# Two-layer hybrid encoder step on one core: second layer's projection ends on values, its raw weights share buffers with the softmax weights, the first head's scores move beside it, cached keys load a block ahead, the sample's steps start later

## The chip, the cores and the metric

The kernel is one program on one core of a Trainium2 chip. The metric is the device time of one execution in microseconds, here the median of three runs. The engines are named as the profile names them: PE (matmul and transpose), DVE (vector), ACT (scalar), POOL, and SP, which here only issues transfers; its queue takes them in order.

## The reference, cut to what matters

The kernel runs two layers of an encoder over 16 meta tokens, 1024 prompt tokens and 32 tokens of a running stream (the sample), 1072 columns of width 1024 in all. Every layer is a mixer and an MLP. The change lies in the second layer's mixer, a forgetting attention with 16 heads of 64:

```python
q, k, v, lf = c_project(hp, w_in_c[i], b_f_c[i], qnorm_c[i], knorm_c[i])   # h @ w_in, q and k normalised per head
xp = xp + fox_prompt(q, k, v, lf) @ w_out_c[i]                              # causal, 1040 keys
q, k, v, lf = c_project(hs, w_in_c[i], b_f_c[i], qnorm_c[i], knorm_c[i])
xs = xs + fox_sample(q, k, v, lf, cache_c_k[i], cache_c_v[i], cache_c_logf[i]) @ w_out_c[i]   # 1024 cached keys + 32
# both: s = q.k * SCALE + c_q - c_k, c = cumsum(log forget);  p = softmax(s);  o = p @ v
```

The arithmetic is float32. A product is made of three matmuls on a high and a low part of each operand (`mm3`), or of two where one stacks both parts.

## The kernel before, in words

**Order of the program.** Layer 1, its MLP, `project_c` (the second layer's projection), `fox` (its attention with the output product), the second MLP. Inside `fox` and the MLPs the order on PE is the order of the code. In `project_c` every engine's order, and everywhere the order on the other engines and of the transfers, comes from a scheduler that runs when the program is built.

**Before the projection.** The last quarter of the columns is normalised at its very end: squares on ACT, sums on DVE and POOL, one matmul with a constant (`normed`, L145), two activations, and then for eight blocks a scaling on DVE (L217), a high part on ACT (L64) and a low part on DVE (L66) or POOL (L68), through four buffers `nm_t`. They lie in a pool that is closed when this is done. `fh0`, the pool of the first head, is opened next, and above it `pc`, the pool of the projection, each on memory that earlier pools have left. A tile's first writer waits for the last readers of what lay there before.

**The projection.** Seven groups of columns of `w_in_c`, in the order of the list `cols`: values of heads 12 to 15 with the forget gates, q and k of heads 0 to 7, two groups of values of six heads, q and k of heads 8 to 15. For each group four transfers bring raw weights (`pj_raw`, three buffers), ACT and DVE split them (`pj_wh`, `pj_wl`), and for each of nine column tiles 24 matmuls go to one of four PSUM banks. Then `post_norm` (q, k: square, reduce, `rstd`, scale, gain on POOL, four transposes, split, out to DRAM) or `post_v` (copy, split, out to DRAM). Step n is group times nine plus tile. At step 9 `forget_sums` makes the running sums of the forget gates: transposes, a scan on DVE, and two halves that are split and sent out, once for the prompt and once for the sample. At step 45 head 0 is loaded, at steps 56, 58, 60, 62 its first four `head_scores` are made (matmuls, `softmax` with max on DVE, exp on ACT, division on POOL).

**The attention.** A head has two quads of four query blocks; quad 0 has 5 steps, quad 1 has 9, so 14 steps a head. A step transposes a block of weights (`head_weights`, L1490) and multiplies the block of two steps before with the values (L1500, L1501). From step 5 on the scores of the next head are made, one a step (L1472, L1473, L1476); in head 0 steps 0 to 3 also make its own scores 4 to 7. The sample's attention is cut into 53 pieces (`smp`), one a step from step 4 of head 0: `keys` loads 512 cached keys into the single buffer `fk_c` and transposes them. Heads 0, 2, ... lie in `fh0`, heads 1, 3, ... in the pool `fh`, which reuses the memory of the projection's pool. Each takes seven transfers for queries and keys (`fh_qa`, `fh_ka`, `fh_qb`, `fh_kb`) and two for values.

Of the kernel before, what the change touches and what calls it, by code (L numbers as in the profile page):

```python
# [8 lines left out]
F32 = mybir.dt.float32  # L9
F32R = mybir.dt.float32r  # L10
# [3 lines left out]
ALU = mybir.AluOpType  # L14
# [4 lines left out]
P = 128  # L19
# [32 lines left out]
class Core:  # L52
# [177 lines left out]
    def project(self, w, cols, sb, hT, lag, part, width=512, bufs=(3, 5)):  # L230
# [3 lines left out]
        for n, (a, b, post, bank) in enumerate(cols):  # L234
            ws = []
            for k in range(0, KB, 2):
                raw = sb.tile([P, 2, width], F32, name="pj_raw", bufs=bufs[0])
                wh = sb.tile([P, 2, width], F32R, name="pj_wh", bufs=bufs[1])
                wl = sb.tile([P, 2, width], F32R, name="pj_wl", bufs=bufs[1])
                nc.sync.dma_start(raw[:, :, :b - a], wv[:, k:k + 2, a:b])  # L240
                self.hi_lo(raw[:, :, :b - a], wh[:, :, :b - a], wl[:, :, :b - a])
                ws += [(wh[:, j, :b - a], wl[:, j, :b - a]) for j in range(2)]
# [936 lines left out]
    def project_c(self, hT, beside):  # L1179
        tc, nc, i, o = self.tc, self.nc, self.i, self.o  # L1180
        with tc.tile_pool(name="pc", bufs=2, reuse_waits="tile") as sb, tc.tile_pool(name="pcp", bufs=4, space=PSUM, reuse_waits="tile") as ps:
# [33 lines left out]
            def post_v(h0, nh, gates):  # L1215
                def post(t, r0, m, pp):
# [6 lines left out]
                    if gates:  # L1223
# [26 lines left out]
                (2048, 2432, post_v(0, 6, False)), (2432, 2816, post_v(6, 6, False)),  # L1250
                (512, 1024, post_norm(gq, self.zq1, 8, None)), (1536, 2048, post_norm(gk, self.zk1, 8, "new_c_k")),
            ]
            steps = self.project(w, [(*c, banks(ps)) for c in cols], sb, hT, 0,
                                 lambda: sb.tile([P, 512], F32, name="hn_sq"), bufs=(3, 4))
            for n, _ in enumerate(steps):
                if n == len(TILES):
                    with tc.tile_pool(name="pf", bufs=1, side="right", reuse_waits="tile") as sf:
                        self.forget_sums(sf)
                if n in beside:
                    beside[n]()  # L1260


    def forget_sums(self, sb):
# [9 lines left out]
        for dst, parts in ((self.cp, prompt), (self.cs, sample)):  # L1273
# [9 lines left out]
            for a in range(0, n, n // 2):  # L1283
                hl = [sb.tile([16, 528], F32R, name=f"fs_{x}")[:, :n // 2] for x in "hl"]
                self.hi_lo(d[:, a:a + n // 2], *hl)
                for x in range(2):
                    nc.sync.dma_start(dst[x, :, a:a + n // 2], hl[x].bitcast(F32))


    def softmax(self, sb, pieces, p, n):  # L1290
        nc = self.nc
        nm = sb.tile([P, 2], F32, name="sm_nm", bufs=4)
        den = sb.tile([P, 2], F32, name="sm_den", bufs=4)
        for j, (s, a, b) in enumerate(pieces):
            nc.vector.tensor_reduce(nm[:, j:j + 1], s, axis=AX.X, op=ALU.max, negate=True)
        if len(pieces) == 2:
            nc.vector.tensor_tensor(nm[:, 0:1], nm[:, 0:1], nm[:, 1:2], op=ALU.min)
        for j, (s, a, b) in enumerate(pieces):
            nc.scalar.activation(p[:, a:b], s, AF.Exp, bias=nm[:, 0:1], accum_out=den[:, j:j + 1])
        if len(pieces) == 2:  # L1300
            nc.vector.tensor_tensor(den[:, 0:1], den[:, 0:1], den[:, 1:2], op=ALU.add)
# [5 lines left out]
    def fox_sample(self, sb, work, ms):  # L1307
# [15 lines left out]

        def keys(g, a, p):
            def go():
# [132 lines left out]
    def head_scores(self, qi, d, sb, ps=None):  # L1458
# [19 lines left out]
        p = sb.tile([P, 1040], F32, name="fx_p1", bufs=6) if qi > 3 else self.fh0.tile([P, 528], F32, name="fx_p0", bufs=4)  # L1478
# [25 lines left out]
    def fox(self, d0, p0, ms, norm):  # L1504
        tc, nc, i = self.tc, self.nc, self.i
        w = i["w_out_c"][0]
        with ExitStack() as st:
# [3 lines left out]
            with tc.tile_pool(name="fh", bufs=2, reuse_waits="tile") as sb, tc.manual_schedule(engines={mybir.EngineType.PE}):  # L1511
# [16 lines left out]
                d, pr = {0: d0}, {(0, 0): p0}  # L1528
# [49 lines left out]
                for u, (h, quad) in enumerate(units):  # L1578
                    for t in range(4 * quad + 5):
                        step = 5 * quad + t  # L1580
                        if h == 14 and step == 0:
                            for n, names in enumerate((("fk_c", "fk_h", "fk_l"), ("fx_s", "fx_cs", "fv_c"))):
                                raw, wh, wo = (ssb.tile([P, 2, 512], F32R if x else F32, name=y, bufs=1) for x, y in enumerate(names))
# [3 lines left out]
                        if h == 0 and step < 4:  # L1587
                            scores(0, 4 + step)
# [3 lines left out]
                        if smp and (h or step >= 4):  # L1592
                            smp.pop(0)()
# [34 lines left out]
def body(tc, i, o):  # L1628
    C = Core(tc, i, o)
    nc = tc.nc  # L1630
    with ExitStack() as st:
# [215 lines left out]
```

## Time and profile before

| | |
|---|---|
| runs, us | 2826.71, 2821.92, 2815.38; median 2821.92 |
| profiled execution, us | 2817.04, span 2815.3 |
| granted PE clock, mean | 0.969 |
| PE / DVE / ACT / POOL busy | 93% / 67% / 45% / 23% |
| projection on PE | 1288.0 to 1607.4 us of the span |
| attention on PE, first to last product with values | 1625.0 to 2051.3 us |

The profiled execution lies 4.88 us below the median of the runs. In rows of the timeline the columns are start and duration in us, engine, line, operation, output and inputs, count, and in brackets the idle time before it and what ended it. In a table by windows, `(x..)` counts instructions and PEclk is the granted clock of PE as a share of full speed.

### The profile page before, as it was taken

The numbers are of one execution on the slowest core, as the hardware profiler recorded it, in microseconds if no ns is written. First come the engines' busy times: TensorE is split into PE (matmuls) and PEld (weight loads), VectorE is DVE, ScalarE is ACT, GpSimd is POOL, SyncE is SP. The second block draws the span as 40 slices with busy tenths as digits, with TensorE's granted clock in tenths as the row PEclk, the third lists the DMA queues.
The fourth block names the chain that finished last, engine by engine and source line by source line (L and its number), as shares of the span: only waits on it lengthen the run. The fifth ranks groups of instructions, "written<-read, shape, count | busy, mean of one in ns | idle before, by whom it ended". The sixth has DMA issues, their size and how long they took to land.

```text
span 2815.3 us, 49213 instructions
## 1 busy us (share of the span) xinstructions
PE 2624.8 (93%) x18391; PEld 2437.4 (87%) x18391; DVE 1892.2 (67%) x3850; ACT 1266.0 (45%) x2833; POOL 634.5 (23%) x693
## 2 busy tenths in 40 slices
PE   5899999869999999999999888999968999999998
PEld 5888988769999899998798766778868999999998
DVE  5934478786766686677634556778788767677553
ACT  4345465443333354545333356666653333335342
POOL 3423365110000211012201244555510000111000
PEclk9999999989999999999999989999989999999999
DMA  6343242225443766544464555444232344586643
GB/s 194 101 134 105 74 149 58 75 87 160 128 155 128 279 207 202 145 132 130 131 207 134 145 144 133 98 101 98 63 92 96 130 154 141 180 269 210 195 142 104
DMA packets 358038, 394.82 MB, mean 140 GB/s; under 512 B 41567, under 2 KB 294200, under 8 KB 355752
## 3 DMA queue, kind: packets, MB, share of 16 engines
q1 hardware_dynamic: 340840, 306.55, 38.2%
q0 software_dynamic: 16960, 85.13, 8.4%
q8 instruction: 145, 2.38, 0.4%
q14 instruction: 93, 0.76, 0.1%
HBM read 264.99 MB, written 125.48 MB: 139 GB/s over the span
## 4 chain that ended last, share of the span: by engine, by line
PE 75%; DVE 11%; DMA 4%; ACT 2%; issue 2%; POOL 1%; SPq 0%; DVEq 0%; ACTq 0%; POOLq 0%
PE bank L75 12%; PE bank L76 12%; PE bank L77 12%; PE mu_y L76 8%; PE mu_y L77 8%; PE mu_y L75 8%; PE bank L1490 3%; PE bank L1500 2%; PE bank L1501 1%; DMA md_ur<-ud 1%; PE fx_s L1472 1%; PE fx_s L1473 1%; PE bank L257 1%; DMA md_raw<-in_w_down 1%; DVE xT L878 1%
## 5 line engine op out<-in xcount | busy, mean ns | idle before, releaser
L75 PE MATMUL bank<-pj_wh,h 128*128 128x384 f32 (+3 forms) x832 | 300.1, 363 | 9.8 <-ACT pj_wh L64 7.4
L77 PE MATMUL bank<-pj_wh,h 128*128 128x384 f32 (+3 forms) x832 | 297.4, 359 | 6.1 <-DVE h L66 4.8
L76 PE MATMUL bank<-pj_wl,h 128*128 128x384 f32 (+3 forms) x832 | 298.5, 360 | 3.0 <-DVE pj_wl L66 2.9
L76 PE MATMUL mu_y<-md_u,md_w 128*128 128x268 f32 (+1 forms) x896 | 259.9, 290 | 13.3 <-DVE md_u L66 11.3
L77 PE MATMUL mu_y<-md_u,md_w 128*128 128x268 f32 (+1 forms) x896 | 259.4, 290 | 6.1 <-POOL md_w L68 6.1
L75 PE MATMUL mu_y<-md_u,md_w 128*128 128x268 f32 (+1 forms) x896 | 260.7, 291 | 0.3 <-ACT md_u L64 0.2
L75 PE MATMUL bank<-md_u,md_w 128*128 128x268 f32 (+1 forms) x896 | 257.3, 287 | 0.0
L76 PE MATMUL bank<-md_u,md_w 128*128 128x268 f32 (+1 forms) x896 | 255.9, 286 | 1.2 <-DVE md_u L66 1.2
L77 PE MATMUL bank<-md_u,md_w 128*128 128x268 f32 (+1 forms) x896 | 255.6, 285 | 0.0
L64 ACT CAST md_u<-md_ur 128x536 fp32r<-128x536 f32 (+1 forms) x224 | 141.6, 636 | 232.0 <-PE mu_y L77 119.6
L66 DVE TENSOR_TENSOR md_u<-md_ur,md_u 128x536 fp32r<-128x536 f32 (+1 forms) x220 | 155.3, 710 | 131.3 <-ACT md_u L64 131.1
L77 PE MATMUL mu_y<-ho_T,mu_w 128*128 128x268 f32 (+1 forms) x768 | 220.0, 286 | 0.0
L76 PE MATMUL mu_y<-ho_T,mu_w 128*128 128x268 f32 (+1 forms) x768 | 219.8, 286 | 0.0
L75 PE MATMUL mu_y<-ho_T,mu_w 128*128 128x268 f32 (+1 forms) x768 | 219.3, 286 | 0.0
L1303 POOL TENSOR_TENSOR fx_p<-fx_p,sm_den 128x144 f32<-128x144 f32 (+7 forms) x128 | 150.6, 1177 | 182.1 <-DVE sm_den L1302 166.6
L66 DVE TENSOR_TENSOR mu_w<-mu_raw,mu_w 128x512 fp32r<-128x512 f32 x160 | 109.6, 687 | 116.9 <-ACT mu_w L64 116.9
L76 PEld LDWEIGHTS mu_y<-md_u,md_w 128*128 128x128 f32 x896 | 172.4, 192 | 15.2 <-DVE md_u L66 12.8
L64 ACT CAST mu_w<-mu_raw 128x512 fp32r<-128x512 f32 x160 | 99.3, 622 | 190.6 <-PE bank L77 124.7
L75 PEld LDWEIGHTS bank<-pj_wh,h 128*128 128x128 f32 x832 | 160.2, 193 | 22.8 <-ACT pj_wh L64 7.9
L77 PEld LDWEIGHTS mu_y<-md_u,md_w 128*128 128x128 f32 x896 | 172.3, 192 | 6.5 <-POOL md_w L68 6.5
L77 PEld LDWEIGHTS bank<-pj_wh,h 128*128 128x128 f32 x832 | 159.8, 192 | 17.6 <-DVE h L66 5.1
L76 PEld LDWEIGHTS bank<-pj_wl,h 128*128 128x128 f32 x832 | 160.3, 193 | 15.9 <-DVE pj_wl L66 4.4
(553 smaller groups left out, 8156.4 us busy)
## 6 DMA issues: line engine op xcount, KB each, us to landing
md_raw<-in_w_down SPq DMA_DIRECT2D x160, 256.0 KB
mu_raw<-in_w_up SPq DMA_DIRECT2D x64, 512.0 KB
ud<-xT POOLq DMA_DIRECT2D x16, 1876.0 KB, 7.5
md_ur<-ud SPq DMA_DIRECT2D x112, 268.0 KB
ud<-xT POOLq DMA_DIRECT2D x16, 1848.0 KB, 10.0
md_ur<-ud SPq DMA_DIRECT2D x112, 264.0 KB
fh_ka<-zk SPq DMA_DIRECT2D x32, 260.0 KB
md_k<-in_w_down SPq DMA_DIRECT2D x8, 1024.0 KB
```

The costliest lines, as they stand in the source:

```text
L64: nc.scalar.copy(hi, src)
L66: nc.vector.tensor_tensor(lo, src, hi.bitcast(F32), op=ALU.subtract)
L75: mm(out, ah, bh, start=start, stop=False)
L76: mm(out, ah, bl, start=False, stop=False)
L77: mm(out, al, bh, start=False, stop=stop)
L257: nc.tensor.matmul(*args, start=k == x == 0, stop=k == KB - 1 and x == 1)
L878: nc.vector.scalar_tensor_tensor(x[:, k], x[:, k], self.gain[:, 2 * self.l + 1, k:k + 1], y, op0=ALU.mult, op1=ALU.mult)
L1303: nc.gpsimd.tensor_tensor(p[:, :n], p[:, :n], den[:, 0:1].to_broadcast([P, n]), op=ALU.mult)
L1472: nc.tensor.matmul(s[:, a:b], qa[:, qc], ka[:, t0 + a:t0 + b], start=True, stop=False)
L1473: nc.tensor.matmul(s[:, a:b], qb[:, qc], kb[:, t0 + a:t0 + b], start=False, stop=ma >= mb)
L1490: nc.tensor.transpose(pt[:m, P * j:P * j + P], pr[j][:, k0:k0 + m], self.ident)
L1500: nc.tensor.matmul(po[:, c], vt[:m, t], th[:m, c], start=t == 0, stop=False)
```

## The change

1. The list `cols` is put in another order: the second group of values (heads 6 to 11) goes last, q and k of heads 8 to 15 before it.
2. Raw weights no longer have their own three buffers. They take turns in four tiles of 1040 columns in `fh0`, `fx_p10` to `fx_p13`, which also hold the softmax weights of query blocks 4 to 7 (`weights_tile`). For heads 1 and later two more such tiles lie in `fh`, six as before in all.
3. All eight `head_scores` of head 0 are made in the projection, at steps 47, 49, 51, 53, 54, 56, 58, 60. The last of them has three pieces, so `softmax` takes any number of pieces. `fox` makes none for head 0.
4. `forget_sums` splits and sends each sum in four quarters through tiles of 264 columns, not in two halves through 528.
5. Cached keys have two buffers, and the transfer of the next block is issued when a block is taken.
6. The sample's pieces start at step 9 of head 0, and heads 1 to 3 take two at steps 0 and 2.

```diff
@@ project
-                raw = sb.tile([P, 2, width], F32, name="pj_raw", bufs=bufs[0])
+                raw = raws() if raws else sb.tile([P, 2, width], F32, name="pj_raw", bufs=bufs[0])
@@ project_c
-                (2048, 2432, post_v(0, 6, False)), (2432, 2816, post_v(6, 6, False)),
+                (2048, 2432, post_v(0, 6, False)),
                 (512, 1024, post_norm(gq, self.zq1, 8, None)), (1536, 2048, post_norm(gk, self.zk1, 8, "new_c_k")),
+
+                (2432, 2816, post_v(6, 6, False)),
...
+                                 raws=lambda: self.weights_tile(self.fh0)[:, 0:1024].rearrange("p (k n) -> p k n", k=2))
...
+    def weights_tile(self, sb):
+        j = self.turn % (4 if sb is self.fh0 else 6)
+        self.turn += 1
+        return (self.fh0 if j < 4 else sb).tile([P, 1040], F32, name=f"fx_p1{j}", bufs=1)
@@ forget_sums
-            for a in range(0, n, n // 2):
-                hl = [sb.tile([16, 528], F32R, name=f"fs_{x}")[:, :n // 2] for x in "hl"]
-                self.hi_lo(d[:, a:a + n // 2], *hl)
+            for a in range(0, n, n // 4):
+                hl = [sb.tile([16, 264], F32R, name=f"fs_{x}")[:, :n // 4] for x in "hl"]
+                self.hi_lo(d[:, a:a + n // 4], *hl)
                 for x in range(2):
-                    nc.sync.dma_start(dst[x, :, a:a + n // 2], hl[x].bitcast(F32))
+                    nc.sync.dma_start(dst[x, :, a:a + n // 4], hl[x].bitcast(F32))
@@ fox_sample
+        def cached(g, a):
+            kc = sb.tile([P, 4, 256], F32, name="fk_c", bufs=2)
+            nc.sync.dma_start(kc, i["cache_c_k"][0, 0, 512 * a:512 * a + 512, 4 * g:4 * g + 4].rearrange("(n p) h d -> p n (h d)", p=P))
+            return kc
+
+        ahead = [cached(0, 0)]
...
-                    kc = st["kc"] = sb.tile([P, 4, 256], F32, name="fk_c", bufs=1)
-                    nc.sync.dma_start(kc, i["cache_c_k"][0, 0, 512 * a:512 * a + 512, h0:h0 + 4].rearrange("(n p) h d -> p n (h d)", p=P))
+                    st["kc"] = ahead.pop()
+                    if g + a < 4:
+                        ahead.append(cached(g + a, 1 - a))
@@ head_scores
-        p = sb.tile([P, 1040], F32, name="fx_p1", bufs=6) if qi > 3 else self.fh0.tile([P, 528], F32, name="fx_p0", bufs=4)
+        p = self.weights_tile(sb) if qi > 3 else self.fh0.tile([P, 528], F32, name="fx_p0", bufs=4)
@@ fox
-                d, pr = {0: d0}, {(0, 0): p0}
+                d, pr = {0: d0}, {(0, 0): p0[:4], (0, 1): p0[4:]}
+                self.turn = 4
...
-                        if h == 0 and step < 4:
-                            scores(0, 4 + step)
...
-                        if smp and (h or step >= 4):
-                            smp.pop(0)()
+                        if smp and (h or step >= 9):
+                            for _ in range(2 if h and step in (0, 2) else 1):
+                                smp.pop(0)()
@@ body
-            C.fh0 = fh0
+            C.fh0, C.turn = fh0, 0
...
-                                  **{56 + 2 * q: lambda q=q: p0.append(C.head_scores(q, d0, fh0)) for q in range(4)}})
+                                  **{n: lambda q=q: p0.append(C.head_scores(q, d0, fh0)) for q, n in enumerate((47, 49, 51, 53, 54, 56, 58, 60))}})
```

The order of instructions moves with it. At the start of the projection, on ACT; `pj_wh` is the high part of the raw weights, `h` that of the normalised columns, L148 to L150 the two activations behind the matmul L145:

```order
 L64 CAST h_13838<-nm_t 128x268 x8
 L134 ACTIVATE nm_t<-xT 128x268 x6
-L64 CAST pj_wh<-pj_raw 128x2x272 x4
 L148 ACTIVATE nm_a<-bank,eps 128x268
 L149 ACTIVATE nm_y<-nm_a 128x268
 L150 ACTIVATE nm_a<-nm_y 128x268
+L64 CAST h_13838<-nm_t 128x268 x8
+L64 CAST pj_wh<-fx_p_14533 128x2x272
+L64 CAST pj_wh<-fx_p_14539 128x2x272
+L64 CAST pj_wh<-fx_p_14545 128x2x272
+L64 CAST pj_wh<-fx_p_14551 128x2x272
```

The split of the first raw weights moved from ahead of the last quarter's normalisation to behind all eight of its blocks.

The transfers on SP at the end of the projection, before; `zk1` and `zv1` are the keys and values going out to DRAM, the `fh_` tiles are head 1's:

```order
L1452 DMA fh_qa_17860<-zq1_76 64x1024 x2
L1202 DMA zk1_77<-pc_t_17625 128x4x128
L1452 DMA fh_ka_17861<-zk1_77 64x1040
L1202 DMA zk1_77<-pc_t_17625 128x4x128
L1452 DMA fh_ka_17861<-zk1_77 64x1040
L1452 DMA fh_qb_17864<-zq1_76 64x1024
L1452 DMA fh_kb_17862<-zk1_77 64x1040
L1452 DMA fh_kb_17862<-cp_79 2x1040
```

and now; `fh_qa_18307` to `fh_kb_18309` are head 2's tiles, in `fh0`, and `fh_qa_17884`, `fh_ka_17885` head 1's:

```order
L1469 DMA fh_qa_18307<-zq1_76 64x1024 x2
L1221 DMA zv1_78<-pc_t_17710 128x768
L1469 DMA fh_ka_18308<-zk1_77 64x1040 x2
L1469 DMA fh_qb_18311<-zq1_76 64x1024
L1469 DMA fh_kb_18309<-zk1_77 64x1040
L1469 DMA fh_kb_18309<-cp_79 2x1040
L1191 DMA out_new_c_v_p<-pc_z_17766 128x384
L1221 DMA zv1_78<-pc_t_17768 128x768
L1469 DMA fh_qa_17884<-zq1_76 64x1024
L1191 DMA out_new_c_v_p<-pc_z_17798 128x384
L1469 DMA fh_qa_17884<-zq1_76 64x1024
L1469 DMA fh_ka_17885<-zk1_77 64x1040
```

Head 2's queries and keys moved ahead of head 1's, which stand between the last tiles of values going out.

More of the change, by code (lines that the diff above doesn't have):

```diff
@@ L226, in scaled, with project @@
         return to
-    def project(self, w, cols, sb, hT, lag, part, width=512, bufs=(3, 5)):
+    def project(self, w, cols, sb, hT, lag, part, width=512, bufs=(3, 5), raws=None):
         nc = self.nc
@@ L1249, in project_c @@
                 (0, 512, post_norm(gq, self.zq1, 0, None)), (1024, 1536, post_norm(gk, self.zk1, 0, "new_c_k")),
-                (2048, 2432, post_v(0, 6, False)), (2432, 2816, post_v(6, 6, False)),
+                (2048, 2432, post_v(0, 6, False)),
                 (512, 1024, post_norm(gq, self.zq1, 8, None)), (1536, 2048, post_norm(gk, self.zk1, 8, "new_c_k")),
+                (2432, 2816, post_v(6, 6, False)),
             ]
             steps = self.project(w, [(*c, banks(ps)) for c in cols], sb, hT, 0,
-                                 lambda: sb.tile([P, 512], F32, name="hn_sq"), bufs=(3, 4))
+                                 lambda: sb.tile([P, 512], F32, name="hn_sq"), bufs=(3, 4),
+                                 raws=lambda: self.weights_tile(self.fh0)[:, 0:1024].rearrange("p (k n) -> p k n", k=2))
             for n, _ in enumerate(steps):
@@ L1282, in forget_sums @@
             nc.vector.tensor_tensor_scan(d, ones.to_broadcast([16, n]), d, 0.0, op0=ALU.mult, op1=ALU.add)
-            for a in range(0, n, n // 2):
-                hl = [sb.tile([16, 528], F32R, name=f"fs_{x}")[:, :n // 2] for x in "hl"]
-                self.hi_lo(d[:, a:a + n // 2], *hl)
+            for a in range(0, n, n // 4):
+                hl = [sb.tile([16, 264], F32R, name=f"fs_{x}")[:, :n // 4] for x in "hl"]
+                self.hi_lo(d[:, a:a + n // 4], *hl)
                 for x in range(2):
-                    nc.sync.dma_start(dst[x, :, a:a + n // 2], hl[x].bitcast(F32))
+                    nc.sync.dma_start(dst[x, :, a:a + n // 4], hl[x].bitcast(F32))
     def softmax(self, sb, pieces, p, n):
         nc = self.nc
-        nm = sb.tile([P, 2], F32, name="sm_nm", bufs=4)
-        den = sb.tile([P, 2], F32, name="sm_den", bufs=4)
+        nm = sb.tile([P, 3], F32, name="sm_nm", bufs=4)
+        den = sb.tile([P, 3], F32, name="sm_den", bufs=4)
         for j, (s, a, b) in enumerate(pieces):
             nc.vector.tensor_reduce(nm[:, j:j + 1], s, axis=AX.X, op=ALU.max, negate=True)
-        if len(pieces) == 2:
-            nc.vector.tensor_tensor(nm[:, 0:1], nm[:, 0:1], nm[:, 1:2], op=ALU.min)
+        for j in range(1, len(pieces)):
+            nc.vector.tensor_tensor(nm[:, 0:1], nm[:, 0:1], nm[:, j:j + 1], op=ALU.min)
         for j, (s, a, b) in enumerate(pieces):
             nc.scalar.activation(p[:, a:b], s, AF.Exp, bias=nm[:, 0:1], accum_out=den[:, j:j + 1])
-        if len(pieces) == 2:
-            nc.vector.tensor_tensor(den[:, 0:1], den[:, 0:1], den[:, 1:2], op=ALU.add)
+        for j in range(1, len(pieces)):
+            nc.vector.tensor_tensor(den[:, 0:1], den[:, 0:1], den[:, j:j + 1], op=ALU.add)
         nc.vector.reciprocal(den[:, 0:1], den[:, 0:1])
@@ L1582, in fox @@
                             for n, names in enumerate((("fk_c", "fk_h", "fk_l"), ("fx_s", "fx_cs", "fv_c"))):
-                                raw, wh, wo = (ssb.tile([P, 2, 512], F32R if x else F32, name=y, bufs=1) for x, y in enumerate(names))
+                                raw, wh, wo = (ssb.tile([P, 2, 512], F32R if x else F32, name=y, bufs=1 + (y == "fk_c")) for x, y in enumerate(names))
                                 nc.sync.dma_start(raw, w.rearrange("(k p) n -> p k n", p=P)[:, 6:8, 512 * n:512 * n + 512])
```

## The prediction

> **What bounds the kernel now.** I read the page first, then PE's busy time by windows, then what PE waited for where it was idle.
>
> ```profile
> span 2815.3 us, 49213 instructions
> PE 2624.8 (93%) x18391; PEld 2437.4 (87%) x18391; DVE 1892.2 (67%) x3850; ACT 1266.0 (45%) x2833; POOL 634.5 (23%) x693
> 1440.00:1500.00 60.00, 60.00 (x346) 59.46 (x345) 15.08 (x24) 21.16 (x41) 0.00 (x0) 1.00 0.61 208
> 1605.00:1657.00 52.00, 36.08 (x151) 26.46 (x150) 23.83 (x53) 22.17 (x53) 20.57 (x20) 0.67 0.71 181
> 1657.00:1770.00 113.00, 101.27 (x612) 78.23 (x611) 79.97 (x180) 75.51 (x169) 53.61 (x46) 0.95 0.46 118
> PE bank L1342 <- DMA fk_c<-in_cache_c_k: 6.3, 2, 3.5
> PE bank L1197 <- POOL pc_z L1209: 4.2, 1, 4.2
> PE bank L1490 <- POOL fx_p L1303: 4.1, 1, 4.1
> ```
>
> PE sets the end. Inside the projection it never idles (60.00 of 60), so only its idle time and its half clock can be won or lost. The 52 us in which the projection turns into the attention are the weak place: PE was busy 36.08 of 52.00, idle 15.9, and its clock stood at 0.67, which costs about 36.08 x 0.33 = 11.9. Together 27.8 us. The next 113 us lose 11.7 idle and 101.27 x 0.05 = 5.1. The three waits are what the change names: the gain of the last keys, the first head's last softmax, the cached keys.
>
> **The change part by part.** PE's work is the same, so I add up gaps.
>
> *A, the first raw weights.* `fx_p10` and `fx_p11` lie where the last normalisation keeps its buffers `nm_t`. In the built program the first raw load waits for that normalisation's low parts of block 4 (DVE) and 5 (POOL), the second for blocks 6 and 7; before, it waited for nothing that late. The order on ACT says the same: `pj_wh` stands behind all eight `h`. So PE does L145 and then waits for the whole chain.
>
> ```profile
> 1285.85 0.28 PE L77 MATMUL bank<-md_u,md_w 128*128 128x268 f32 x1
> 1288.03 0.53 PE L75 MATMUL bank<-pj_wh,h 128*128 128x272 f32 x2 [1.90 <-ACT pj_wh L64]
> 1291.23 0.43 PE L77 MATMUL bank<-pj_wh,h 128*128 128x272 f32 x1
> 1292.26 0.29 PE L77 MATMUL bank<-pj_wh,h 128*128 128x272 f32 x1
> 1293.00 0.61 PE L145 MATMUL bank<-nm_acc,mean 128*128 128x268 f32 x2
> 1287.67 0.44 DVE L136 TENSOR_TENSOR nm_acc<-nm_acc,nm_t 128x268 f32<-128x268 f32 x1
> 1296.16 1.72 DVE L217 SCALAR_TENSOR_TENSOR nm_t<-xT,gain,nm_y 128x268 f32<-128x268 f32 x4
> 1274.55 1.72 DVE L217 SCALAR_TENSOR_TENSOR nm_t<-xT,gain,nm_y 128x268 f32<-128x268 f32 x4
> 1276.20 0.71 DVE L66 TENSOR_TENSOR md_u<-md_ur,md_u 128x536 fp32r<-128x536 f32 x1
> 1280.40 1.93 DVE L66 TENSOR_TENSOR h<-nm_t,h 128x268 fp32r<-128x268 f32 x2
> 1280.18 1.84 POOL L68 TENSOR_TENSOR h<-nm_t,h 128x268 fp32r<-128x268 f32 x2 [1.23 <-ACT h L64]
> 1288.77 4.59 SPq L240 DMA_DIRECT2D pj_raw<-in_w_in_c  x4
> 1291.56 0.65 ACT L64 CAST pj_wh<-pj_raw 128x544 fp32r<-128x544 f32 x1 [2.49 <-DMA pj_raw<-in_w_in_c]
> ```
>
> In times of this trace: the last L136 ends at 1288.1, L139 and a small scaling follow, L145 starts at 1288.75. From L145 to the first L217 the old run took 1296.16 - 1293.00 = 3.2 with 0.1 of other work, so L217 starts at 1291.8. From there to the low parts of blocks 4 and 5 the quarter before took from 1274.55 to about 1281.4, 6.85 with 0.71 of MLP work in it; DVE's own nine or ten pieces of 0.43 with two waits need 4.9. I take 5.5: 1297.3. Issue to split took 1291.56 - 1288.77 = 2.8, the split 0.65: PE starts at 1300.75 where it started at 1288.03, 12.7 later, less 0.4 because L145 interrupts nothing afterwards. At the start a 272-wide matmul comes every 0.23 us at half clock, later every 0.125 (rows 1288.03 to 1292.26), so the old start lost 1.7 us; after a longer gap I take 2.2. A = +12.8, from 11 (4.9 and a load of 2.2) to 15.5 (6.85, a load of 3.5, a longer half clock). A fourth buffer gives nothing back, since PE waits for no raw weights later.
>
> *B, quarters in the running sums.* Here PE stood once.
>
> ```profile
> 1360.97 0.80 PE L75 MATMUL bank<-pj_wh,h 128*128 128x512 f32 x1 [2.33 <-DVE pc_z L278]
> 1366.26 0.63 PE L75 MATMUL bank<-pj_wh,h 128*128 128x512 f32 x1
> 1367.27 0.39 PE L75 MATMUL bank<-pj_wh,h 128*128 128x512 f32 x1
> 1352.22 0.63 ACT L64 CAST fs_h<-fs_d 16x520 fp32r<-16x520 f32 x1 [1.64 <-DVE fs_d L1282]
> 1354.52 0.63 ACT L64 CAST fs_h<-fs_d 16x520 fp32r<-16x520 f32 x1 [1.32 <-DMA cp<-fs_h]
> 1355.97 0.74 ACT L1280 ACTIVATE fs_d<-bank 16x128 f32<-16x128 f32 x4 [0.81 <-DVE fs_l L66]
> ```
>
> Each piece waits until the one before has landed (1.32 of idle ACT), since the tile is single, and ACT's next work (four `fs_d`) waits for the last piece. Two pieces took 1352.22 to 1355.97, 3.75. Four pieces of about 0.4 with three landings of some 1.7 from issue take about 7.2: 3.45 later. But the built order puts the transposes that feed the scan 9 or 10 of the 0.23 us matmuls earlier against the place where PE stalls, which gives 2.3 back. B = +1.2, from 0 to 4. The eight extra small transfers sit on SP where PE has its weights already. The second sum's pieces hide in ACT's waits on PE.
>
> *C, the new order of groups and head 0's scores.* The same instructions, moved into stretches where DVE and ACT are half idle (the window 1440 to 1500, in a values group, has DVE 15.08 and ACT 21.16 of 60). The gain on POOL no longer stands at the end (4.2), nor the softmax (4.1). Nothing added; if that cover were missing, four softmaxes of about 2 us of ACT and DVE would show as PE idle here.
>
> *D, the start of the attention.* Call the end of the projection E. Steps 0 to 4 need weights made long before. Step 5 needs head 1's queries and keys, whose memory is the projection's: its first load waits for E itself, as before, but now head 2's load stands ahead of it, and the last values between.
>
> ```profile
> 1607.03 0.39 PE L77 MATMUL bank<-pj_wh,h 128*128 128x512 f32 x1
> 1607.45 1.36 SPq L1452 DMA_DIRECT2D fh_qa<-zq  x2
> 1611.32 6.45 DMA fh_qb<-zq
> 1610.00:1615.00 5.00, 2.24 (x9) 1.72 (x9) 2.37 (x6) 1.08 (x2) 1.26 (x1) 0.77 1.10 284
> 1620.00:1625.00 5.00, 4.95 (x19) 3.78 (x19) 0.37 (x1) 1.69 (x4) 1.53 (x3) 0.50 1.00 230
> fh_ka<-zk SPq DMA_DIRECT2D x32, 260.0 KB
> fh_qa<-zq SPq DMA_DIRECT2D x32, 256.0 KB
> zv<-pc_t SPq DMA_DIRECT2D x16, 384.0 KB
> out_new_c_v_p<-pc_z SPq DMA_DIRECT2D x16, 192.0 KB
> ```
>
> One head's queries and keys are six transfers of 256 to 260 KB, 1.6 MB; a tile of values puts out 0.6 MB. With DMA full the core moved 230 to 284 GB/s, middle 257. Head 2's load may start when head 0's last scores are made, two value tiles before E; a tile is 24 matmuls of 60.00/346 = 0.173, so at E - 8.4. Until E that is 2.8 MB, 10.8 us of traffic in 8.4; then 2.2 MB, 8.5 us. Head 1 is there at E + 9.4 to E + 10.8; I take 10 (a single transfer took 6.45 in the same crowd, which agrees). Steps 0 to 4 end at about E + 4.3: eleven transposes, then three splits of ACT 0.6 and DVE 0.7 behind two leftover tiles of values. Idle: 1.5 in those steps, 5.7 at step 5, 1 for the rest. The clock falls: after B's 2.33 us it stood at half from 1360.97 to 1366.7, and a matmul came every 0.43 instead of 0.23, so 5.7 us lose 2.6; with the slack steps before, 3.3. That is 11.5 in place of 27.8: D = -16.3, from -21 (head 1 there by E + 6) to -9 (E + 14, and half clock as long as before).
>
> The cached keys' first block is issued about E + 7 and wanted at step 9, about E + 17; the sample's queries land about there too. DVE's copy of the selector (L1324) waits for a transfer issued at about E + 5.5 and stands ahead of step 5's maxima: hidden behind head 1's load, and if that came early it would be the next wait. The 6.3 us on cached keys go away because the sample starts later and a buffer is ahead.
>
> [...]
>
> *F, more sample work per step.* Heads 1 to 3 carry 48 of the 53 pieces in place of 42; DVE was busy 79.97 of 113 there, so they fit, but two pieces in one step want PSUM banks together. +1, from -3 (no wait left on cached keys) to +5.
>
> Sum: 12.8 + 1.2 - 16.3 + 1.0 = -1.3 on the profiled 2817.04. That run lies 4.9 under the median of 2821.92; against the median it gives 2820.6, and I say **2820**.
>
> **The rivals.**
>
> *The attention's start loses nearly nothing, and later heads gain too (faster).* If head 1's load were there by step 5, all of 27.8 but about 5 is won, and 4 of the later 11.7 idle: 12.8 + 1.2 - 22.8 - 4 = -12.8; with A at its lower end -14.6: 2807. For it: the cached keys and the softmax are the named releasers. Against: 1.6 MB of another head are ahead on the same queue. Chance 0.22, with the third rival below.
>
> *Head 1's load comes late (slower).* At the 181 GB/s of the window 1605 to 1657, 2.8 MB need 15.3 us, 6.9 of them behind E, and 2.2 MB another 12.1: E + 19. PE then idles 14.7 at step 5, and the clock stays at half as it did until 1640: 1.5 + 14.7 + 1 + 9 = 26 in place of 27.8. 12.8 + 1.2 - 1.6 + 2 = +14.4: 2836. It decides from E + 18 on. Against it: DMA did reach 284 when asked. Chance 0.11.
>
> *The raw loads don't wait (A is zero).* Then -14.1, 2808. The order on ACT and the shared memory speak against it. It is counted in the first rival's chance; both at once would give -12.8 - 12.8 = -25.6, 2796.
>
> **How the numbers follow.** The forecast has 0.67. A measurement of this kernel can tell about 0.5%, 14 us, from no change; the forecast's own terms stay within it at nearly all their ends. Added up, the ends are -13 and +15.5, so 2809 to 2837, and the runs shown spread 11 us. The range is 2802 to 2835: below it takes in the first rival and half the way to its joining with the third. Faster by over 0.5%: 0.22; within: 0.67; slower: 0.11.
>
> **What would show each step.** A: a PE gap of about 14 us before the first L75 of the projection, released by `pj_wh`, and the first raw load on SP issued only behind the last L66 and L68 on `h`; a gap under 5 would refute it. B: PE's wait on `pc_z` L278 of 2 to 6 us once. D: no wait on `pc_z` L1209 nor on cached keys, one gap of 4 to 7 us at the first L1489 released by `fh_kb` or `fh_ka`, half clock for some 10 us behind it. F: PE busy at 100 to 103 of the 113 us behind. The forecast is wrong if the gap at step 5 is above 15 or absent, or if the projection now stalls inside.

## The result, and the profile after

| | before | changed |
|---|---|---|
| median of 16 runs each, us | 2821.03 (2813.17 to 2826.71) | 2829.1 (2822.53 to 2834.86) |
| ratio, 95% interval | | 1.0034 (1.0025 to 1.0042) |
| profiled execution, us | 2817.04 | 2822.53 |

The change costs 0.34%, less than the 0.5% that the prediction called no change, but its interval excludes no change, and it lies on the other side of zero than the forecast of 2820. The profiled executions lie 4.0 and 6.6 us below their medians and 5.5 us apart; the medians lie 8.1 apart.

The page of the changed kernel shows the same PE work as before (2624.8 busy), in a longer span:

```profile
span 2820.8 us, 49270 instructions
PE 2624.3 (93%) x18377; PEld 2437.3 (86%) x18391; DVE 1896.4 (67%) x3866; ACT 1268.6 (45%) x2845; POOL 633.6 (22%) x693
```

What PE waited for between 1270 and 1780 us, in total, times, longest:

```profile
PE bank L75 <- ACT pj_wh L64: 12.1, 1, 12.1
PE fx_s L1489 <- DMA fh_ka<-zk: 5.6, 1, 5.6
PE bank L1359 <- DVE fk_l L66: 3.0, 3, 1.4
PE bank L1391 <- ACT fx_s L1380: 2.8, 2, 1.9
PE bank L145 <- DVE nm_acc L139: 2.6, 1, 2.6
PE bank L75 <- DVE pc_z L278: 2.3, 1, 2.3
PE fx_s L1490 <- DMA fh_kb<-zk: 2.3, 1, 2.3
```

The waits on the gain, on the softmax and on the cached keys are gone. In their place stand one long wait for the first split raw weights, and two for head 1's keys. L1359 and L1391 belong to the sample; the 13 further rows of the view have 2.2 us or less each.

To see what came after them I cut both traces by work, not by time: from 30 us ahead of the projection's last matmul to the first product with values of head 1 (the 15th of the attention's pairs), and from there through heads 1 to 3 to the 65th pair, in head 4. By the order of the code the second stretch begins behind the sample's pieces of step 2 of head 1, so it holds 40 of the 53 pieces before and 43 now. The columns are the window, its length, the busy time of PE, PEld, DVE, ACT, POOL with their counts, the granted clock, the DMA share and GB/s. Before:

```profile
1577.30:1673.40 96.10, 78.55 (x377) 60.38 (x375) 48.51 (x116) 41.14 (x100) 35.73 (x32) 0.82 0.60 158
1673.40:1792.40 119.00, 106.49 (x638) 82.68 (x639) 85.30 (x197) 78.12 (x177) 59.67 (x52) 0.94 0.45 116
```

Changed:

```profile
1595.40:1666.50 71.10, 60.46 (x345) 51.30 (x343) 35.37 (x84) 36.78 (x90) 24.08 (x21) 0.93 0.74 207
1666.50:1798.40 131.90, 116.69 (x662) 90.12 (x662) 87.40 (x203) 79.89 (x181) 61.39 (x53) 0.90 0.40 105
```

Idle time is the length less PE's busy time; "cold" is PE's busy time multiplied by one less the clock. Where PE idles at half clock, this counts a little twice, so it serves to compare and not to add up to the last tenth. Each figure comes from one trace.

| idle + cold, us | before | changed | difference |
|---|---|---|---|
| head 0 and the end of the projection | 17.5 + 14.1 = 31.7 | 10.6 + 4.2 = 14.9 | -16.8 |
| heads 1 to 3 | 12.5 + 6.4 = 18.9 | 15.2 + 11.7 = 26.9 | +8.0 |

So the start of the attention won what was forecast (-16.3), the projection's start lost what was forecast, and heads 1 to 3 gave away 8 us where the forecast had 1.

### The profile page after: what moved, and what is told of

It is laid out like the page before. It is cut to its first block, busy times and chain, and to the rows that moved or that the text cites. A ratio compares the mean times of both kernels' runs of the same rounds, so it can differ in the third digit from the quotient of the medians.

```text
span 2820.8 us, 49270 instructions
## 1 busy us (share of the span) xinstructions
PE 2624.3 (93%) x18377; PEld 2437.3 (86%) x18391; DVE 1896.4 (67%) x3866; ACT 1268.6 (45%) x2845; POOL 633.6 (22%) x693
## 4 chain that ended last, share of the span: by engine, by line
PE 75%; DVE 11%; DMA 3%; ACT 2%; issue 2%; SPq 1%; POOL 1%; DVEq 0%; ACTq 0%; POOLq 0%
PE bank L75 13%; PE bank L77 12%; PE bank L76 12%; PE mu_y L76 8%; PE mu_y L77 8%; PE mu_y L75 8%; PE bank L1507 2%; PE bank L1517 2%; PE bank L1518 1%; PE fx_s L1489 1%; PE bank L257 1%; PE fx_s L1490 1%; DVE xT L878 1%; DMA md_ur<-ud 1%; DVE md_w L66 1%
## 5 line engine op out<-in xcount | busy, mean ns | idle before, releaser
L75 PE MATMUL bank<-pj_wh,h 128*128 128x384 f32 (+3 forms) x832 | 299.7, 362 | 19.8 <-ACT pj_wh L64 17.0
L76 PE MATMUL mu_y<-md_u,md_w 128*128 128x268 f32 (+1 forms) x896 | 259.6, 290 | 13.0 <-DVE md_u L66 10.8
L77 PEld LDWEIGHTS bank<-pj_wh,h 128*128 128x128 f32 x832 | 159.1, 191 | 17.3 <-DVE h L66 4.2
```

Of the source, the lines that this page charges most:

```text
L75: mm(out, ah, bh, start=start, stop=False)
L76: mm(out, ah, bl, start=False, stop=False)
L77: mm(out, al, bh, start=False, stop=stop)
```

## The experiments

All ratios are to the kernel before, run on the same chip: 16 runs of the changed kernel, 4 to 12 of each other. The chips differ; the kernel before has medians from 2818.87 to 2821.29 on them, so a difference of two medians is good to about 2 us, and the ratios decide.

The expectations give the "loss" of heads 1 to 3 by another count than the table (36.7 for the kernel before, 43.3 for both): the length of the stretch less some 82 to 87 us for its matmuls, a figure whose source is not on record. Only differences compare with the table's.

| kernel | median, us | ratio, 95% interval | idle + cold in heads 1 to 3 |
|---|---|---|---|
| changed | 2829.1 | 1.0034 (1.0025 to 1.0042) | 15.2 + 11.7 |
| raw tiles above `fh0` | 2816.79 | 0.9987 (0.9977 to 0.9998) | 16.2 + 10.4 |
| one piece a step | 2827.0 | 1.0025 (1.0013 to 1.0037) | 17.3 + 5.7 |
| both | 2810.38 | 0.9962 (0.9949 to 0.9975) | 18.2 + 4.5 |
| both, start at step 4 | 2809.28 | 0.9962 (0.9947 to 0.9976) | 12.9 + 3.1 |
| raw tiles above, ten pieces in head 0 | 2808.14 | 0.9956 (0.9944 to 0.9968) | 12.2 + 7.5 |
| changed, start at step 4 | 2822.16 | 1.0009 (0.9999 to 1.0018) | 12.8 + 3.1 |
| before, start at step 9 | 2825.52 | 1.002 (1.0004 to 1.0035) | 19.3 + 11.8 |
| raw tiles above, doubles at steps 5 to 9 | 2821.75 | 1.0009 (0.9995 to 1.0023) | 22.7 + 9.5 |
| raw tiles above, start in head 1 | 2819.71 | 0.9995 (0.9982 to 1.0008) | 16.3 + 9.3 |
| both, head 0's scores as before | 2820.2 | 1.0008 (0.9997 to 1.0019) | 16.3 + 11.8 |
| both, head 1's load in two parts | 2817.49 | 0.9988 (0.9971 to 1.0005) | 16.4 + 11.9 |
| changed, transfers in the order of the code | 2849.51 | 1.01 (1.0086 to 1.0115) | 19.8 + 13.0 |

### The raw weights' place

```diff
-        return (self.fh0 if j < 4 else sb).tile([P, 1040], F32, name=f"fx_p1{j}", bufs=1)
+        return (self.fr if j < 4 else sb).tile([P, 1040], F32, name=f"fx_p1{j}", bufs=1)
@@ body
-        with tc.tile_pool(name="fh0", bufs=1, reuse_waits="tile") as fh0:
+        with tc.tile_pool(name="fh0", bufs=1, reuse_waits="tile") as fh0, tc.tile_pool(name="fr", bufs=1, reuse_waits="tile") as fr:
```

> The changed kernel, with one part undone: the four tiles fx_p10 to fx_p13, which the raw weights use, lie in a pool of their own above fh0 (from address 50720 in place of 18848), so the first raw load no longer overlaps the buffers of the last normalisation. Same bytes in all. Theory (the raw loads wait for the normalisation, term A = 12.8): PE starts the projection within 3 us of the matmul L145 again, the 12.1 us wait on pj_wh shrinks to about 2, and the time falls by 11 to 14 us, from 2829.1 to about 2816.5, a ratio to the kernel before of 0.998. Rival (the gap comes from something else in the change, for instance four raw transfers at once on the DMA engines): the gap stays near 12 us and the ratio at 1.003.

First the chain in the changed kernel, in rows of the timeline (the last low parts of the normalisation on DVE and POOL, the raw loads, the split, PE):

```profile
1295.87 1.88 DVE L66 TENSOR_TENSOR h<-nm_t,h 128x268 fp32r<-128x268 f32 x2
1295.65 1.80 POOL L68 TENSOR_TENSOR h<-nm_t,h 128x268 fp32r<-128x268 f32 x2 [0.82 <-ACT h L64]
1296.93 7.03 SPq L240 DMA_DIRECT2D fx_p<-in_w_in_c  x7
1299.85 0.65 ACT L64 CAST pj_wh<-fx_p 128x544 fp32r<-128x544 f32 x1 [3.45 <-DMA fx_p<-in_w_in_c]
1300.54 0.82 PE L75 MATMUL bank<-pj_wh,h 128*128 128x272 f32 x2 [12.05 <-ACT pj_wh L64]
1303.66 0.43 PE L76 MATMUL bank<-pj_wl,h 128*128 128x272 f32 x1
1304.11 0.29 PE L75 MATMUL bank<-pj_wh,h 128*128 128x272 f32 x1
```

With the tiles above `fh0`, where the loads go out ahead of the normalisation:

```profile
1283.59 2.88 SPq L240 DMA_DIRECT2D fx_p<-in_w_in_c  x4
1291.37 0.73 PE L75 MATMUL bank<-pj_wh,h 128*128 128x272 f32 x2 [1.90 <-ACT pj_wh L64]
```

The wait falls from 12.05 to 1.90 and the time by 12.3 us. The rival falls: four raw buffers and four transfers at once are still there. The whole of this wait came from which old buffers the new tiles lie on.

### One piece of the sample a step

```diff
-                            for _ in range(2 if h and step in (0, 2) else 1):
-                                smp.pop(0)()
+                            smp.pop(0)()
```

> The changed kernel, but never two pieces of the sample in one step: one a step from step 9 of head 0, so that six of the 53 pieces fall into head 4. Theory (in heads 1 to 3 two pieces at steps 0 and 2 stand one behind the other without the next head's scores between them, so their waits on DVE, ACT and the sample's queries come bare): of the loss that heads 1 to 3 have gained, some 9 us in the two traces, 5 to 9 go; the time is 2820 to 2824, a ratio of 0.9998 to 1.001. Rival (the loss comes from the later start and the second buffer of cached keys, whatever the pieces per step): within 2 us of 2829, a ratio of 1.0027 to 1.0041.

> The first two edits together: raw weights' tiles above fh0, one sample piece a step. What is left of the change is the order of the groups, head 0's scores in the projection, the quarters, the cached keys ahead and the later start. If the terms add: 2829.1 - 12.8 - 7 = 2809, a ratio of 0.996 (0.9945 to 0.997). If the pieces are not the cause: 2816, 0.998.

Heads 1 to 3, one piece a step:

```profile
1664.40:1794.70 130.30, 113.04 (x671) 87.18 (x671) 89.92 (x207) 82.45 (x185) 61.62 (x53) 0.95 0.43 111
```

and with the raw tiles above `fh0` as well:

```profile
1652.10:1782.50 130.40, 112.19 (x670) 86.14 (x670) 89.66 (x207) 82.58 (x185) 61.62 (x53) 0.96 0.43 111
```

Alone it won 2 us, on top of the moved tiles 6.4, and the two intervals allow a common value between. Its 2827.0 lies at the edge of what the rival gave. In the traces idle time did not fall (17.3 and 18.2, against 15.2, with 45 pieces in the stretch in place of 43); only the clock was better. Two pieces in one step are therefore at most a part of the loss, and the theory as I wrote it, that the pairs wait bare, is not borne out by the idle time.

### The start of the sample

```diff
-                        if smp and (h or step >= 9):
-                            for _ in range(2 if h and step in (0, 2) else 1):
-                                smp.pop(0)()
+                        if smp and (h or step >= 4):
+                            smp.pop(0)()
```

With the raw tiles above `fh0`:

> The raw tiles above fh0 and one sample piece a step, as in the run of both, but the pieces start at step 4 of head 0 as in the kernel before, not at step 9. Theory (phase: in the changed kernel other pieces fall on steps 0 to 4 of a head, where no scores of the next head stand between them; above all the keys and the first weights behind a sample softmax): the loss of heads 1 to 3, 36.7 before and 43.3 in the run of both, falls back to 36 to 38; in head 0 five more pieces cost 2 to 5 at the wait for head 1's load and the first cached keys. Together 2806 to 2811, a ratio of 0.9948 to 0.9965. Rival (a piece costs about the same wherever it falls, and five pieces more in heads 1 to 4 are what costs): heads 1 to 3 keep 41 or more, and what head 0 gains is lost there: 2810 to 2814.

With the raw tiles left where the change put them, the sixth part of the change undone and nothing else:

> The changed kernel with its sixth part alone undone: the sample's pieces start at step 4 of head 0 again, one a step. The raw tiles stay where the change put them, so the 12 us at the projection's start stay too. Theory (the sample's later, denser steps are what the forecast priced at +1 and what cost some 8): with the raw tiles moved, going from the change's steps to the start at step 4 went from 2816.8 to 2809.3; here 2829.1 should fall by as much, to 2820 to 2823, a ratio of 0.9997 to 1.0007, with 15 to 20 us of idle and cold clock in heads 1 to 3 in place of 27.8, and some 5 more in head 0. Rival (that difference was chance, and the steps of the sample cost about nothing): 2826 to 2830, a ratio of 1.002 to 1.0036.

And the other way round, the kernel before with only the start moved from step 4 to step 9:

> The kernel before with one edit: the sample's pieces start at step 9 of head 0 in place of step 4, one a step, with the single buffer of cached keys. It shows the start alone. Theory (moving five pieces out of head 0 and shifting the phase costs some 6 to 7 us in heads 1 to 4, whatever else changed): the loss of heads 1 to 3 goes from 36.7 to 42 to 44, while head 0 no longer waits 6.3 us for the first cached keys: about as before, a ratio of 0.998 to 1.001. Rival (the cost comes from the second buffer of cached keys or from the other edits): heads 1 to 3 stay at 36 to 38 and the time falls by 4 to 7 us, a ratio of 0.9975 to 0.9985.

Heads 1 to 3 with the raw tiles above and the start at step 4:

```profile
1660.60:1777.90 117.30, 104.42 (x638) 80.47 (x639) 85.01 (x197) 78.19 (x177) 59.80 (x52) 0.97 0.44 114
```

The change with its sixth part undone:

```profile
1676.60:1793.70 117.10, 104.27 (x638) 80.50 (x639) 85.02 (x196) 77.83 (x177) 59.76 (x52) 0.97 0.44 113
```

The kernel before, started at step 9:

```profile
1666.30:1804.10 137.80, 118.49 (x671) 91.31 (x671) 89.77 (x207) 82.47 (x185) 61.66 (x53) 0.90 0.43 108
```

Undoing the sixth part of the change takes 6.9 us off the changed kernel (1.0034 to 1.0009 in ratios), and 7.5 with the tiles moved (0.9987 to 0.9962). Both medians came out as expected. Both traces of the start at step 4 give the same 16 us in heads 1 to 3, less than before. The late start alone, in the kernel before, raises heads 1 to 3 from 18.9 to 31.2, while the stretch ahead of them falls from 31.7 to 25.6. That trace is of the slowest of its ten runs (2833.70), but the median too rose, by 0.2%, where 0.998 to 1.001 was expected. So the cost belongs to the steps of the sample; the second buffer of cached keys is not its cause. Part of it is mere number: three more pieces in the stretch (43 in place of 40) at 18.9/40 = 0.47 each are 1.4.

Head 0 pays some of it back: with the early pieces PE waits there for the first cached keys instead of for head 1's load.

```profile
PE bank L1359 <- DMA fk_c<-in_cache_c_k: 11.8, 1, 11.8
1598.10:1676.60 78.50, 64.17 (x369) 54.62 (x367) 36.94 (x90) 39.18 (x94) 26.09 (x23) 0.91 0.70 195
```

Its idle and cold time is 20.1 (14.3 + 5.8) in place of 14.9. So about 5 of the 16.8 us that the attention's start had won came from the sample's later start, and in the same two traces heads 1 to 3 pay 10.9 for it (26.9 against 16.0).

### Which pieces stand where

Three kernels ask why the later steps cost more. All have the raw tiles above `fh0`.

```diff
 ten in head 0:
                         if smp and (h or step >= 9):
+                            for _ in range(1 if h else 2):
 doubles at steps 5 to 9:
+                        if smp and step >= (5 if h else 9):
+                            for _ in range(2 if h and step < 10 else 1):
...
 from step 3 of head 1:
+                        if smp and (h > 1 or h and step >= 3):
```

> The raw tiles above fh0, pieces from step 9 of head 0, and in the heads behind none at steps 0 to 4 but two at steps 5 to 9 and one at steps 10 to 13: 14 a head. Theory (cover: a piece hides its waits where the next head's scores are made): heads 1 to 3 lose 36 to 40 in place of 45.7 (doubles at steps 0 and 2) and 43.3 (singles), 2803 to 2808, a ratio of 0.994 to 0.996. Rival (what costs is two pieces in one step, since both want a PSUM bank and DVE, wherever they stand): heads 1 to 3 lose 45 or more, 2813 to 2818, a ratio of 0.998 to 0.999.

> The raw tiles above fh0, and ten pieces of the sample in head 0, two a step at steps 9 to 13, then one a step: from head 1 on each piece stands at the step of the kernel before (and of the start at step 4), but head 0's steps 4 to 8 have none. Theory (phase): heads 1 to 3 lose 34 to 38 as with the start at step 4 (34.9), in place of 43.3; head 0, which has ten pieces in five steps behind the load of head 1, loses 18 to 22 in place of 16.1 (start at step 9) and 22.6 (start at step 4): 2804 to 2809, a ratio of 0.9942 to 0.9957. Rival (the two-in-a-step pieces cost about 1 us each step, and a piece costs the same in any phase): heads 1 to 3 stay at 40 or more and the ratio at 0.996 or above.

> The raw tiles above fh0, one piece a step from step 3 of head 1: a group of heads has 13 pieces and a head 14 steps, so every later group meets the steps at which the kernel before has the group ahead of it. Theory (phase): the loss per piece is that of the kernel before and the start at step 4, so heads 1 to 3 with 39 pieces lose 33 to 37 and head 4 with 14 pieces about 6 to 7 more than its usual 5.6; head 0, with none, 13 to 15. Altogether 2803 to 2808, a ratio of 0.994 to 0.9955. Rival (no phase; each piece costs 0.5 to 0.6 wherever it stands): the sum is that of the run of both, 2809 to 2812, a ratio of 0.996.

Doubles at steps 5 to 9:

```profile
1647.40:1788.90 141.50, 118.79 (x683) 91.17 (x684) 92.49 (x207) 83.28 (x188) 62.82 (x54) 0.92 0.43 108
```

Ten in head 0:

```profile
1660.40:1780.40 120.00, 107.75 (x638) 83.61 (x639) 85.41 (x197) 78.14 (x177) 59.78 (x52) 0.93 0.43 110
```

From step 3 of head 1:

```profile
1643.70:1776.40 132.70, 116.44 (x677) 89.17 (x677) 88.36 (x201) 85.30 (x188) 61.95 (x52) 0.92 0.47 119
```

The theory of cover falls: with the doubles beside the next head's scores heads 1 to 3 lose 32.2, the most of these, and the time, 2821.75, is above what either side gave. The theory of phase (it matters which piece meets which step) holds as far as the idle time goes: every kernel whose pieces meet the steps of the kernel before idles 12.2 to 12.9 there (before, start at step 4 twice, ten in head 0), every other one 15.2 to 22.7. But the first four also have the fewest pieces in the stretch, 40, and the others 43 to 50. At the 12.5/40 = 0.31 of the kernel before, number alone gives 13.4 for 43 pieces, 14.1 for 45, 15.0 for 48 and 15.6 for 50, so it accounts for a third of the rise in the changed kernel (15.2) and for most of it in the start in head 1 (16.3 with 50 pieces); of the doubles' 22.7 it leaves 7.7. The start in head 1 was meant to have the same phase one group later. Up to 1738 us, near the end of head 3, it idled 9.7 of 94.3 us; from there to 1776.4, where the last group of pieces has another length, 6.6 of 38.4 at a clock of 0.87, and it missed its forecast. And the phase hardly shows in the whole time: 2810.4, 2809.3 and 2808.1 for both, start at step 4 and ten in head 0 have overlapping intervals, since what heads 1 to 3 win is paid in head 0 (13.4, 19.2 and 18.7 of idle and cold time). That phase adds idle time beyond the number of pieces is thus supported, not isolated: no run changes the phase and keeps the number in the stretch. By which of the chained waits it does so was not tried.

### Head 0's scores

```diff
+                        if h == 0 and step < 4:
+                            scores(0, 4 + step)
...
-enumerate((47, 49, 51, 53, 54, 56, 58, 60))
+enumerate((56, 58, 60, 62))
```

> As the run of both (raw tiles above fh0, one piece a step from step 9), but head 0's scores as in the kernel before: blocks 0 to 3 late in the projection (steps 56 to 62), 4 to 7 in steps 0 to 3 of the attention. The groups of columns keep the new order. Theory (the scores' move is worth the softmax wait, 4.1 us with half clock, while the values at the end of the projection are worth the 4.2 us on the gain): head 0's loss rises from 16.1 to 20 to 25, less what the scores hide of the wait for head 1's load: 2812 to 2818, a ratio of 0.9975 to 0.999. Rival (head 1's load sets step 5 whatever is made before it): head 0's loss stays at 15 to 18, and the time at 2809 to 2812, a ratio of 0.996.

PE's waits at steps 0 and 5, in rows of the timeline:

```profile
1611.55 0.38 PE L1507 MATMUL bank<-ident,fx_p 128*16 128x128 f32 x1 [2.78 <-POOL fx_p L1312]
...
1627.68 0.38 PE L1507 MATMUL bank<-ident,fx_p 128*16 128x128 f32 x1 [3.61 <-POOL fx_p L1312]
```

The first stretch, from 30 us ahead of the projection's last matmul, in the run of both and here:

```profile
1584.80:1652.10 67.30, 58.58 (x337) 50.50 (x335) 33.20 (x80) 34.68 (x86) 24.09 (x21) 0.92 0.74 210
1576.70:1657.20 80.50, 70.97 (x369) 60.15 (x367) 34.32 (x75) 37.09 (x87) 25.90 (x24) 0.83 0.67 183
```

The softmax waits are back, PE no longer waits for head 1's load, and the time is 9.8 us higher (0.9962 to 1.0008 in ratios), more than the 2812 to 2818 that were expected. In head 0 the trace has 21.6 us of idle and cold time in place of 13.4. Making the first head's eight scores inside the projection is the part of the change that pays: what is left without it, with the raw tiles moved and one piece a step, comes to 1.0008 (0.9997 to 1.0019). The new order of groups, the quarters and the second buffer of cached keys were not tried alone.

### Head 1's load

```diff
-tc.manual_schedule(engines={mybir.EngineType.PE}):
+tc.manual_schedule(engines={mybir.EngineType.PE, mybir.EngineType.SP}):
```

> The changed kernel, with SP's transfers of the attention in the order of the code, so that head 1's queries and keys stand ahead of head 2's. Theory (head 2's load ahead on the queue delays head 1's): the waits on fh_ka and fh_kb at step 5, 5.6 + 2.3 us, fall to 2 to 4 together, head 1's keys land 6 to 8 us after the projection's last matmul in place of 9.6 and 12.3, and the time falls by 4 to 7 us to about 2823.5 (ratio 1.001) if no later transfer suffers. Rival (the load's own 1.6 MB and the last values set the landing, whatever stands ahead): the waits stay at 7 to 9 us and the ratio at 1.003.

First the changed kernel: its last projection matmul, the first issue of head 1's load, and the two waits:

```profile
1625.18 0.34 PE L77 MATMUL bank<-pj_wh,h 128*128 128x384 f32 x1
...
1634.92 0.46 PE L1489 MATMUL fx_s<-fh_ka,fh_qa 128*128 128x144 f32 x1 [5.56 <-DMA fh_ka<-zk]
1637.69 0.46 PE L1490 MATMUL fx_s<-fh_kb,fh_qb 66*128 66x144 f32 x1 [2.30 <-DMA fh_kb<-zk]
```

```profile
1625.55 0.45 SPq L1469 DMA_DIRECT2D fh_qa<-zq  x1
```

With the transfers in the order of the code:

```profile
1638.70 1.10 SPq L1469 DMA_DIRECT2D fh_qa<-zq  x2
```

```profile
1649.58 0.46 PE L1489 MATMUL fx_s<-fh_ka,fh_qa 128*128 128x144 f32 x1 [14.18 <-DMA fh_ka<-zk]
```

The edit failed as an improvement: the sample's constants and cached keys, which the code names first, now stand ahead of head 1's load, and it is issued 7.3 us after PE begins the attention in place of 0.2. Without head 2's 1.6 MB ahead the load still took 1649.58 - 1638.70 = 10.9 us to the first scores (0.5 MB of cached keys were ahead of it), against 1634.92 - 1625.55 = 9.4 in the changed kernel. So taking head 2's load away did not make it faster. That does not settle the question, since other transfers took its place: in the windows between issue and first scores the DMA engines stood at a busy share of about 1 in both traces and moved about 2.5 MB here and 2.9 MB in the changed kernel, in place of head 1's own 1.6 MB.

The other edit was to send the columns of the first two blocks ahead of the rest:

```diff
+            for a, b in ((0, 272), (272, src.shape[-1])) if h == 1 else ((0, src.shape[-1]),):
+                parts[a > 0].append((dst[:, a:b].bitcast(F32), src[:, a:b]))
```

> As the run of both, with head 1's queries and keys sent in two parts, columns 0 to 271 of all six transfers first, then the rest: the scores of blocks 0 and 1 need the first part alone. Theory (step 5 waits for the bytes of head 1's own load, 1.6 MB with DMA full): the first part is there 4 to 6 us after the projection's end in place of 9.5 and 12.3, and the 8 us of waits at step 5 become 1 to 3 there and 2 to 4 at step 7; 2 to 5 us are won: 2805 to 2808, a ratio of 0.9945 to 0.9958. Rival (the queue of issues and head 2's load ahead set the landing): the first part lands no earlier than 8 us after the end, and the time stays at 2810 (0.9962) or gets worse by the seven extra transfers.

```profile
1624.48 0.46 PE L1493 MATMUL fx_s<-fh_ka,fh_qa 128*128 128x144 f32 x1 [3.25 <-DMA fh_ka<-zk]
1629.90 0.46 PE L1494 MATMUL fx_s<-fh_kb,fh_qb 66*128 66x144 f32 x1 [4.97 <-DMA fh_kb<-cp]
```

A quarter of the bytes came 7.3 us after PE had begun the attention in place of 9.6 in the run of both, between what the theory (4 to 6) and the rival (8 or more) gave, so the bytes of the load alone do not set the landing either. Then the second wait, on a small transfer of sums that the scheduler had put behind the cached keys, took the gain, and the median is 7 us above that of both. What sets head 1's landing stays open between its own bytes and the crowd on the DMA engines.

## Why the prediction was right or wrong

**A was right, in place, size and reason.** The first load was forecast free at 1297.3 and went out at 1296.93; PE was forecast at 1300.75 and started at 1300.54, after gaps of 2.58 and 12.05 where about 14 were named. Moving the tiles away took 12.3 us off, against 12.8 forecast (1.0034 to 0.9987 in ratios, 13 us).

**B was right within its error.** The wait on `pc_z` L278 is 2.3 in both traces, where 1.2 more was forecast; the waits of the transposes that feed the scan went from 0.9 to 1.6. That the quarters cost what the earlier transposes gave fits this, but no run shows the two apart. The half clock behind this wait, which the prediction put at 5.7 us, was read from the matmuls; the granted clock stood at half for 6.8 us, 1360.1 to 1366.9, in the first half of which PE was partly idle (last section).

**C was right.** The gain and the softmax left PE's path without a new wait in the projection, and bringing the scores back brings two waits of 2.78 and 3.61.

**D had the right sum, and part of its reason is open.** Head 1's keys let PE go 9.6 us after it began the attention where 10 was forecast, with 5.56 + 2.30 of idle where 5.7 was. The stretch lost 14.9 in place of 31.7: -16.8 against -16.3. The step let head 2's load and the values ahead delay head 1's by up to 2.4 us (10.8 us of traffic in 8.4), and with head 2's load behind it the landing was no faster; whether it delays at all is not shown. About 5 of the 16.8 come from the sample's later start. The step did count that gain: the 6.3 us on cached keys are in its 27.8 and were said to go away. What the prediction lacked is the return of such waits in the heads that the pieces moved to, which is the next step.

**F failed, and it turned the sign.** "They fit" was argued from DVE's 79.97 busy of 113, and +1 (-3 to +5) was taken for banks. Undoing the sixth part alone is worth 6.9 us, beyond the +5; in the traces heads 1 to 3 went from 12.5 + 6.4 to 15.2 + 11.7. That DVE is 70% busy over a stretch says nothing of the chains in it: there PE waits 0.2 to 1.9 us at a time, mostly for the sample's splits, copies and queries, and the moved pieces brought more such waits, by their number and, it seems, their phase. The larger part of the 8 us, 5.3, is not waiting but cold clock, which the term did not price at all. Its size in one trace may be partly luck (last section), but over all runs the changed kernel's granted clock has a mean of 0.9654, and 0.9675 with the sixth part undone; with the tiles moved it is 0.9667 against 0.9706 from step 4. PE was busy 99.05 of the window 1657 to 1770, below the 100 to 103 named.

**The sum.** With the window's own figures, A at 12.3 (gaps of 14.6 in place of 1.9, less 0.4 for L145, which now interrupts nothing), B at 0 to 1, D at -16.8 and F at 8.0 make 3.5 to 4.5; the profiled executions differ by 5.5. In medians the parts close as well: +12.3 for A, +6.9 for the sample's steps, and 0.9962 for what remains when both are undone, -10.7, give +8.5; measured 8.1. Of the rivals, neither of the faster ones (head 1's load in time, raw loads that don't wait) nor the slower one (head 1's load at 19 us) came; the loss came from a term that had no rival at all.

**A version better than both** is what remains when the two losses are taken out: 0.9962, 0.9962 and 0.9956 with the three placements of the sample's pieces, some 11 to 12 us below the kernel before.

## What to carry to other kernels

Where a tile takes its place in memory decides whom its first transfer waits for (12.05 us of PE waiting against 1.90 here): look at what lay at the address, and place early-needed tiles on memory that is free early. When work is moved out of a stall, count its own waits where it lands, and the cold clock behind them (2.7 and 5.3 us more here, in heads 1 to 3); spare busy time of an engine is no price for that. And when a forecast sums to zero out of large terms of both signs, the small term that was waved through decides the sign.

## What the runs showed of the hardware that was not expected

The same PE instructions in heads 1 to 3 met quite different clocks. In the run of both they idled 18.2 us at a clock of 0.96. With head 0's scores as before, same pieces at the same steps:

```profile
1657.20:1791.90 134.70, 118.42 (x670) 91.23 (x670) 90.12 (x207) 82.67 (x185) 61.76 (x53) 0.90 0.40 108
```

they idled 16.3 at 0.90: less waiting, and 11.8 us of cold clock in place of 4.5. So the sum of the waits does not explain it.

In slices of 0.1 us the granted clock of the kernel before and of the changed kernel is either full or half, slices with a change apart. It has 14 and 16 changes between 1285 and 1800 us, and within each of the two traces they lie whole multiples of 3.413 us apart, to 0.02 us. Heads 1 to 3 stood at half clock for 13.7 us before (4 times 3.41) and for 27.3 in the changed kernel (8 times); from the lengths and clocks of the rows, taking the clock for full or half there too, I estimate some 10 us for the run of both and some 27 with head 0's scores as before. That the place of the waits between these points of 3.41 us made the same ones cost more or less is a guess of mine; no run moves the waits against these points alone. The stall on `pc_z` L278 in the kernel before, in stretches between the points:

```profile
1356.64:1360.06 3.42, 1.59 (x12) 0.96 (x11) 2.83 (x2) 2.05 (x9) 0.00 (x0) 1.00 0.12 32
1360.06:1363.47 3.41, 2.50 (x6) 2.02 (x7) 3.41 (x7) 1.07 (x4) 2.47 (x2) 0.51 0.59 133
1363.47:1366.88 3.41, 3.41 (x10) 2.64 (x9) 1.86 (x8) 0.63 (x1) 0.05 (x1) 0.50 0.45 93
1366.88:1370.30 3.42, 3.42 (x19) 2.77 (x18) 0.26 (x1) 0.75 (x2) 0.00 (x0) 0.99 0.04 10
```

The clock fell behind a stretch in which PE was busy 1.59 of 3.42 us, stayed down behind one of 2.50, and came back behind a full one. In the two traces between 1285 and 1800 us, the 15 falls stand behind stretches in which PE was busy 0 to 76%, but behind nine others of 60 to 75% the clock stayed full; the 15 returns stand behind stretches of 90 to 100%, but behind one of 100% and one of 99% it stayed at half. PE's busy time alone thus did not tell when the clock changed here.

In the changed kernel the clock stood at half behind the gap of 12.05 us until 1304.1, 3.6 us after PE started. In the kernel before it came back 5.9 us after PE resumed behind the stall of 2.33 us, at 1366.9; in the stretch ahead of that fall PE had idled 1.8 us (the rows above).
